# The 64-to-128 step of the triangular inverse in one PSUM bank: three rounds of four matrices instead of two bursts of eight

## The chip, the cores and the metric

The kernel runs on one core of a Trainium2 chip. Its metric is the device time of one execution in microseconds. Before the change three runs gave a median of 1597.19 us (1596.48 to 1598.59).

## The reference

One layer of a decoder for 256 tokens of width 2048, in float32. A condition vector gives shift, scale and gate; the normed input `h` is multiplied by one wide matrix `W_in`, and its columns go to two branches:

```
h = RMSNorm_pre(x) * (1 + scale) + shift
[gdn_qkv | gdn_a | gdn_b | gdn_z | ml_qk | ml_v | ml_i | ml_f | ml_o | ml_z | g_A | g_B] = h W_in
y_A = W_pA( RMSNorm_head(GatedDeltaNet(conv(q, k, v), decay, beta)) * silu(gdn_z) )
y_B = W_pB( sigmoid(ml_o) * RMSNorm_head(mLSTM(conv(q, k), v, i, f)) * silu(ml_z) )
out = (sigmoid(g_A) * y_A + sigmoid(g_B) * y_B) W_out
x <- x + gate * RMSNorm_post(out)
```

The change is in the gated delta net (32 value heads of 128, 16 query/key heads). For each head and chunk a unit lower triangular system is solved:

```
lower = where(strict, (k beta) k^T * decay, 0)
sol   = triangular_solve(lower + I, [v beta | k beta exp(g_cum)])
```

The kernel computes the inverse of such a matrix and multiplies with it. It works on chunks of 128 tokens, so the matrix is 128x128. Inverse means here: 32-blocks by substitution, then blocks of 64 from those, then the 128x128 from its two 64-blocks A and B on the diagonal and the block C that couples them, where the new block is −B⁻¹ C A⁻¹. The last is two products of 64x64 for each matrix.

## The kernel before, in words

**The stream.** Nearly all work of TensorE (PE) is products of `h` with weights that are read once. A weight unit is a 1 MB load `raw` on SP's queue (L164, three buffers). It is used in two pieces of 128x1024: ACT rounds each to `whi` (L169), DVE (POOL for some early ones) makes `wlo` = raw − whi (L170), with a ring of four pieces, and PE multiplies in three terms (hi·hi, hi·lo, lo·hi; `mm3`, L227). In a `pt` stretch these are 24 matmuls of 256 columns to a step, in a `pn` stretch 12 of 512.

**The side work.** After each piece, a step, `Side.step()` lets every side generator issue its next piece of work. All engines take their work in the order in which the program issues it; a tile scheduler adds the semaphores. The generators that matter here, for each group of four heads (`zg` 0 to 7, eight matrices of 128x128 in a group):

- `gdn_stage1` (twice per group): convolution and SiLU of q and k (`conv_silu`: ACT L651, DVE L657); load of the decay rows `gb` on SP (L675); masks on POOL (L682, L704); exponentials on ACT (L690–692); Gram products `psa`, `psb` on PE; norms and scaled matrices `au` on DVE (L738–749); the coupling values written out as `ud` (L773).
- `base_inverse`: 32-blocks by substitution on DVE, a chain of L800 (products), L804 (reduction) and L806 for 16 pairs of rows; then the result goes out to DRAM and back in another arrangement: one store `xd` (L809) and, once it has landed, four loads `xcmp` (L813), all on SP's queue. Five steps later DVE transposes and copies it (L817, L822), and ACT copies it (L820) into `x0`, `y0`.
- `gdn_stage2`: products `mp` and `mx` (32-blocks to 64), then the two products of this change: `mq` (L872), for eight matrices one burst from rows 0–63 into PSUM partitions 64–127, which ACT negates into `p2` (L874); a step later `mz` (L881), from rows 64–127 into partitions 0–63, which ACT copies into `x0` (L882). Then `pa`, `pb`, `pc`, `po` use the inverse.

While group zg is in `gdn_stage2`, `base_inverse` of the next group and `gdn_stage1` run beside it.

**What sets the order.** A number, `side.debt`, is the planner's account of DVE time that has been issued beside the stream. Each step takes 1.6 off it, never below zero; work adds to it (1.45 for a channel of the convolution) or gives back where PE's burst takes longer than usual. `base_inverse` asks `side.room(us)` before each of its L800 and L804, which yields step after step until the debt leaves room:

```python
STEP_US = 1.6
ROOM_US = 2.5
    def step(self):
        self.debt = max(0.0, self.debt - STEP_US)
    def room(self, us):
        while self.debt > 0 and self.debt + us > ROOM_US:
            yield
        self.debt += us
```

Four PSUM banks (`gtile`, tag "g") are shared by the side work; `banks(n)` yields until the next n are free, `gfree` gives one back.

Of the kernel before, what the change touches and what calls it, by code (L numbers as in the profile page):

```python
# [9 lines left out]
AF = mybir.ActivationFunctionType  # L10
# [107 lines left out]
def hybrid_layer_kernel(  # L118
# [25 lines left out]
    V, A, T, G, SP = nc.vector, nc.scalar, nc.tensor, nc.gpsimd, nc.sync  # L144
# [53 lines left out]
    def gtile(nm, held=False):  # L198
        i = slots[0] % 4
        slots[0] += 1  # L200
        t = pg.tile([P, 512], F32, name=nm, tag="g")
        freed[i] = 1 << 30 if held else side.t + 1
        slots[1][id(t)] = i, t
        return t

    def gfree(t):
        freed[slots[1].pop(id(t))[0]] = side.t

    def banks(n):

        while any(freed[(slots[0] + j) % 4] >= side.t for j in range(n)):
            yield
# [16 lines left out]
    side = Side()  # L229
# [546 lines left out]
    def base_inverse(zg, res, zr):  # L776
# [48 lines left out]
        while zg < 7 and side.t < res["t"] + STAGE2_STEPS - 1:  # L825
            yield
        side.add(gdn_stage2(zg, res, zr), 0)

    def gdn_stage2(zg, res, zr):
# [3 lines left out]
        def um(m):  # L833
            return au[m // 4][:, m % 4 // 2, 256 + 384 * (m % 2):384 + 384 * (m % 2)]
# [8 lines left out]
        for m in range(8):  # L843
            for t in range(2):
                r, o = 64 * t, 64 * t + 32
                T.matmul(pss[t][o:o + 32, m * 32:(m + 1) * 32], um(m)[r:r + 32, o:o + 32], yc[r:r + 32, m],
                         start=True, stop=True)
# [8 lines left out]
        for m in range(8):  # L856
            T.matmul(psx[0][32:64, S + m * 32:S + (m + 1) * 32], xc[32:64, m], pc_[32:64, m], start=True, stop=True)
            for t in (1, 0):
                r, o = 64 * t, 64 * t + 32
                T.matmul(psx[t][r:r + 32, m * 32:(m + 1) * 32], pc_[o:o + 32, m], xc[o:o + 32, m],  # L860
                         start=True, stop=True)
        A.activation(y0[32:64, :, 0:32], cols32(psx[0], S)[32:64], AF.Copy, scale=-1.0)
        for t in range(2):
            r = 64 * t
            A.activation(x0[r:r + 32, :, r + 32:r + 64], cols32(psx[t])[r:r + 32], AF.Copy, scale=-1.0)
            gfree(psx[t])
        yield
        yield from banks(1)
        psp = gtile("mq", True)
        side.debt -= 1.0  # L870
        for m in range(8):
            T.matmul(psp[64:128, m * 64:(m + 1) * 64], um(m)[0:64, 64:128], y0[:, m], start=True, stop=True)  # L872
        p2 = bp.tile([P, 8, 64], F32, name="p2", tag="p2", bufs=1)
        A.activation(p2[64:128], psp[64:128].rearrange("p (m i) -> p m i", m=8), AF.Copy, scale=-1.0)  # L874
        gfree(psp)
        yield
        yield from banks(1)
        psz = gtile("mz", True)
        side.debt -= 1.0
        for m in range(8):  # L880
            T.matmul(psz[0:64, m * 64:(m + 1) * 64], p2[64:128, m], x0[64:128, m, 64:128], start=True, stop=True)  # L881
        A.copy(x0[0:64, :, 64:128], psz[0:64].rearrange("p (m i) -> p m i", m=8))  # L882
        gfree(psz)
        yield

        rr = res["rr"].rearrange("p b z (h d) -> p b (z h d)", h=2)
        ys = bp.tile([P, 2, 512], F32, name="ys", tag="ys", bufs=1)
# [587 lines left out]
```

## Time and profile before

| what | us |
|---|---|
| median of three runs | 1597.19 |
| the profiled execution | 1597.11 |
| its span (first to last instruction) | 1595.1 |
| PE busy | 1581.4 |
| DVE, ACT, POOL busy | 1146.5, 937.1, 250.6 |

The granted clock of TensorE is 0.998 over the span. The rows of a timeline give start and length of an instruction (or of a run of equal ones, with their count) in us from the span's start, its engine, its line, operation, and the tile that it writes and those it reads, with types and shapes. In square brackets stands the engine's idle time just before, and what ended it. SPq is SP's queue: the length is that of issuing the transfer, not of the transfer. The table of windows has, for each stretch, its length, the busy time (and count of instructions) of PE, PE's weight loads, DVE, ACT and POOL, the granted clock, the mean share in which the 16 DMA engines were busy, and the GB/s.

The side work of one group takes some 81.6 us: the `gb` loads that the second and third group's base inverse have ahead of POOL's masks are issued at 576.26 and 657.89 us, the next at 739.51.

### The profile page before, as it was taken

Reading aid. Unit: us, or ns where it says so; the run is one execution under the profiler, and the core shown is the slowest. Engines: PE = TensorE matmul, PEld = TensorE weight load, DVE = VectorE, ACT = ScalarE, POOL = GpSimd, SP = SyncE. Lnnn points to the kernel's source line nnn. Section 1 sums busy time; section 2 is a strip of 40 time slices with the busy share of each in tenths; the row PEclk is TensorE's granted clock in tenths of the full one; section 3 lists DMA queues with packets and bytes.
Section 4 is the critical chain, followed back from the end, with each engine's and each line's share of the span. In section 5 each row is a group of like instructions: output and inputs, shape, how many; then the busy total and the mean of one; then the engine's idle time right before and its main releaser. Section 6 shows DMA issues by size and latency. Waiting matters only on the chain.

```text
span 1595.1 us, 25488 instructions
## 1 busy us (share of the span) xinstructions
PE 1581.4 (99%) x9854; PEld 1389.0 (87%) x9854; DVE 1146.5 (72%) x1804; ACT 937.1 (59%) x1494; POOL 250.6 (16%) x206
## 2 busy tenths in 40 slices
PE   8999999999999999999999999999999999999998
PEld 5888888899999999999999999889988878888886
DVE  6776556765689788888878888775768766756654
ACT  7755446765666575757576766665566554444443
POOL 5787761000000010000000000000000000100100
PEclk9999999999999999999999999999999999999999
DMA  9998775965565546555646465546778878766573
GB/s 378 393 387 320 268 295 181 297 234 181 189 190 188 189 156 206 167 182 171 193 159 207 154 195 174 187 165 232 279 268 308 320 275 295 282 248 236 206 274 108
DMA packets 96067, 372.37 MB, mean 233 GB/s; under 512 B 26021, under 2 KB 45877, under 8 KB 58185
## 3 DMA queue, kind: packets, MB, share of 16 engines
q1 hardware_dynamic: 95848, 370.65, 66.4%
q8 instruction: 77, 1.26, 0.3%
q14 instruction: 44, 0.36, 0.1%
q0 software_dynamic: 96, 0.09, 0.0%
q10 hardware_dynamic: 2, 0.01, 0.0%
HBM read 354.40 MB, written 16.31 MB: 232 GB/s over the span
## 4 chain that ended last, share of the span: by engine, by line
PE 84%; issue 12%; DMA 1%; POOL 1%; ACT 0%; DVE 0%; SPq 0%; DVEq 0%; ACTq 0%; POOLq 0%
PE pn L227 37%; PE pt L227 29%; PE py L227 8%; POOL mg L1265 1%; PE psa L227 1%; DMA raw<-in_dram 1%; PE mz L881 1%; PE mq L872 1%; PE csil L297 0%; PE po L922 0%; PE pa L893 0%; PE po L921 0%; PE pc L911 0%; PE po L919 0%; PE pb L901 0%
## 5 line engine op out<-in xcount | busy, mean ns | idle before, releaser
L170 DVE TENSOR_TENSOR wlo<-raw,whi 128x1024 fp32r<-128x1024 f32 x451 | 554.2, 1237 | 264.1 <-ACT whi L169 262.6
L169 ACT CAST whi<-raw 128x1024 fp32r<-128x1024 f32 x516 | 532.2, 1046 | 308.1 <-PE pn L227 154.4
L227 PE MATMUL pt<-h_hi,whi 128*128 128x256 f32 x1280 | 367.8, 287 | 0.0
L227 PE MATMUL pt<-h_hi,wlo 128*128 128x256 f32 x1280 | 362.1, 283 | 0.0
L227 PE MATMUL pt<-h_lo,whi 128*128 128x256 f32 x1280 | 362.0, 283 | 0.0
L227 PE MATMUL pn<-whi,h_hi 128*128 128x512 f32 x896 | 353.0, 394 | 0.3 <-ACT h_hi L169 0.3
L227 PE MATMUL pn<-wlo,h_hi 128*128 128x512 f32 x896 | 349.4, 390 | 1.5 <-POOL wlo L170 1.5
L227 PE MATMUL pn<-whi,h_lo 128*128 128x512 f32 x896 | 349.2, 390 | 0.0
L227 PEld LDWEIGHTS pt<-h_hi,whi 128*128 128x128 f32 x1280 | 245.3, 192 | 1.4
L227 PEld LDWEIGHTS pt<-h_lo,whi 128*128 128x128 f32 x1280 | 245.4, 192 | 0.3
L227 PEld LDWEIGHTS pt<-h_hi,wlo 128*128 128x128 f32 x1280 | 245.2, 192 | 0.0
L227 PEld LDWEIGHTS pn<-wlo,h_hi 128*128 128x128 f32 x896 | 168.4, 188 | 36.6 <-POOL wlo L170 2.7
L227 PEld LDWEIGHTS pn<-whi,h_hi 128*128 128x128 f32 x896 | 168.3, 188 | 35.4 <-ACT h_hi L169 1.1
L227 PEld LDWEIGHTS pn<-whi,h_lo 128*128 128x128 f32 x896 | 168.2, 188 | 35.4
L170 POOL TENSOR_TENSOR wlo<-raw,whi 128x1024 fp32r<-128x1024 f32 (+1 forms) x65 | 150.2, 2321 | 47.8 <-ACT whi L169 47.6
L227 PE MATMUL py<-whi,yhi 128*128 128x512 f32 x384 | 150.7, 392 | 0.0
L227 PE MATMUL py<-whi,ylo 128*128 128x512 f32 x384 | 149.6, 390 | 0.0
L227 PE MATMUL py<-wlo,yhi 128*128 128x512 f32 x384 | 149.5, 389 | 0.0
L473 DVE TENSOR_TENSOR part<-pn,part 128x512 f32<-128x512 f32 x112 | 73.8, 686 | 45.5 <-PE pn L227 45.3
L169 ACT CAST yhi<-ya 128x512 fp32r<-128x512 f32 x48 | 29.9, 622 | 127.8 <-PE py L227 110.9
L657 DVE SCALAR_TENSOR_TENSOR qs<-pt,gcv,qs 128x255 f32<-128x255 f32 (+2 forms) x192 | 92.2, 480 | 4.6
L170 DVE TENSOR_TENSOR ylo<-ya,yhi 128x512 fp32r<-128x512 f32 x48 | 33.2, 691 | 75.4 <-ACT yhi L169 75.4
(269 smaller groups left out, 1810.6 us busy)
## 6 DMA issues: line engine op xcount, KB each, us to landing
raw<-in_dram SPq DMA_DIRECT2D x259, 1024.0 KB
ar<-in_dram SPq DMA_DIRECT2D x31, 1024.0 KB
raw<-in_dram SPq DMA_DIRECT2D x16, 512.0 KB
ya<-o_dr SPq DMA_DIRECT2D x32, 256.0 KB
gate_dr<-part SPq DMA_DIRECT2D x11, 512.0 KB
gb<-rows SPq DMA_DIRECT2D x20, 256.0 KB
raw<-in_dram SPq DMA_DIRECT2D x6, 768.0 KB
ug<-ud SPq DMA_DIRECT2D x32, 128.0 KB
```

The source lines that it names most:

```text
L169: A.copy(hi, src)
L170: (eng or V).tensor_tensor(lo, src, hi.bitcast(F32), op=ALU.subtract)
L227: T.matmul(ps, l, r, start=start and i == 0, stop=stop and i == 2, skip_group_check=True)
L473: V.tensor_tensor(part[g][:, b], ps[b], part[g][:, b], op=ALU.add)
L657: V.scalar_tensor_tensor(dst[:, n, sh:], src[:, 0:S - sh], taps(n, 3 - sh), dst[:, n, sh:], op0=ALU.mult, op1=ALU.add)
L872: T.matmul(psp[64:128, m * 64:(m + 1) * 64], um(m)[0:64, 64:128], y0[:, m], start=True, stop=True)
L881: T.matmul(psz[0:64, m * 64:(m + 1) * 64], p2[64:128, m], x0[64:128, m, 64:128], start=True, stop=True)
L1265: G.tensor_tensor(mcols(b, hf, cg), mcols(b, hf, cg), s_, op=ALU.add)
```

## The change

The two bursts become three rounds, a step apart, all in one bank `mqz` that is held until the last. Round 0 has the first products (`mq`) of matrices 0 to 3. Round 1 alternates second products (`mz`) of matrices 0 to 3 with first products of matrices 4 to 7. Round 2 has the second products of matrices 4 to 7. ACT evacuates halves: four instructions of 64x256 instead of two of 64x512. The account `side.debt` gets 0.5 back in each of three rounds instead of 1.0 in each of two. One `yield` more stands in `gdn_stage2`, so `pa` and what follows it there come one step later.

```diff
-        psp = gtile("mq", True)
-        side.debt -= 1.0
-        for m in range(8):
-            T.matmul(psp[64:128, m * 64:(m + 1) * 64], um(m)[0:64, 64:128], y0[:, m], start=True, stop=True)
+        psq = psz = gtile("mqz", True)
         p2 = bp.tile([P, 8, 64], F32, name="p2", tag="p2", bufs=1)
-        A.activation(p2[64:128], psp[64:128].rearrange("p (m i) -> p m i", m=8), AF.Copy, scale=-1.0)
-        gfree(psp)
-        yield
-        yield from banks(1)
-        psz = gtile("mz", True)
-        side.debt -= 1.0
-        for m in range(8):
-            T.matmul(psz[0:64, m * 64:(m + 1) * 64], p2[64:128, m], x0[64:128, m, 64:128], start=True, stop=True)
-        A.copy(x0[0:64, :, 64:128], psz[0:64].rearrange("p (m i) -> p m i", m=8))
-        gfree(psz)
-        yield
+        for i in range(3):
+            side.debt -= 0.5
+            first, second = slice(4 * i, 4 * i + 4), slice(4 * i - 4, 4 * i)
+            for m in range(4 * i, 4 * i + 4):
+                if i > 0:
+                    T.matmul(psz[0:64, (m - 4) * 64:(m - 3) * 64], p2[64:128, m - 4], x0[64:128, m - 4, 64:128],
+                             start=True, stop=True)
+                if i < 2:
+                    T.matmul(psq[64:128, m * 64:(m + 1) * 64], um(m)[0:64, 64:128], y0[:, m], start=True, stop=True)
+            if i > 0:
+                A.copy(x0[0:64, second, 64:128], psz[0:64].rearrange("p (m i) -> p m i", m=8)[:, second])
+            if i < 2:
+                A.activation(p2[64:128, first], psq[64:128].rearrange("p (m i) -> p m i", m=8)[:, first], AF.Copy,
+                             scale=-1.0)
+            if i == 2:
+                gfree(psq)
+            yield
```

After the edit `mz` is L877 and `mq` L880, and the lines after the loop carry numbers greater by 4. Where the middle round lies in PE's order, in the third group: before, a burst of `mz` at that place, between the stream's `pt` and the Gram products `psa`:

```order
L227 MATMUL pt_6823<-h_hi,whi 128x256
L227 MATMUL pt_6823<-h_lo,whi 128x256
L227 MATMUL pt_6823<-h_hi,wlo 128x256
L881 MATMUL mz<-x_2798,p_6927 64x64 x8
L227 MATMUL psa<-qh 128x512
L227 MATMUL psa<-ql,qh 128x512
```

The same place now, where that burst has become pairs:

```order
L227 MATMUL pt_6825<-h_hi,wlo 128x256
L877 MATMUL mqz<-x_2798,p_6921 64x64
L880 MATMUL mqz<-y_2799,au 64x64
L877 MATMUL mqz<-x_2798,p_6921 64x64
L880 MATMUL mqz<-y_2799,au 64x64
...
L227 MATMUL psa<-qh 128x512
```

In the last listing two more such pairs are left out. The eight matmuls stand where `mz` x8 stood; the four first products are where `mq` x8 was, 24 stream matmuls ahead, and the last four follow 24 stream matmuls behind the Gram products.

On DVE, the end of the next group's `base_inverse` among the convolutions (L657) and the stream's `wlo` (L170), before:

```order
L800 TENSOR_TENSOR tmp<-xx,ug 128x8x32
L804 TENSOR_REDUCE xx<-tmp 128x8
L170 TENSOR_TENSOR wlo<-raw,whi 128x1024
L657 SCALAR_TENSOR_TENSOR qs<-pt_5833,gcv,qs 128x255
L657 SCALAR_TENSOR_TENSOR qs<-pt_5833,gcv,qs 128x254
L657 SCALAR_TENSOR_TENSOR qs<-pt_5833,gcv,qs 128x253
L170 TENSOR_TENSOR wlo<-raw,whi 128x1024
L938 SCALAR_TENSOR_TENSOR so<-so,eq 128x8
L657 SCALAR_TENSOR_TENSOR qs<-pt_5834,gcv,qs 128x255
L657 SCALAR_TENSOR_TENSOR qs<-pt_5834,gcv,qs 128x254
L657 SCALAR_TENSOR_TENSOR qs<-pt_5834,gcv,qs 128x253
L170 TENSOR_TENSOR wlo<-raw,whi 128x1024
```

The same stretch now, from the row ahead of the second of those `wlo`:

```order
L800 TENSOR_TENSOR tmp<-xx,ug 128x8x32
L170 TENSOR_TENSOR wlo<-raw,whi 128x1024
L657 SCALAR_TENSOR_TENSOR qs<-pt_5835,gcv,qs 128x255
L657 SCALAR_TENSOR_TENSOR qs<-pt_5835,gcv,qs 128x254
L657 SCALAR_TENSOR_TENSOR qs<-pt_5835,gcv,qs 128x253
L804 TENSOR_REDUCE xx<-tmp 128x8
L170 TENSOR_TENSOR wlo<-raw,whi 128x1024
L942 SCALAR_TENSOR_TENSOR so<-so,eq 128x8
```

The second listing's first `wlo` is the second of the first listing. (Tile numbers differ between the kernels: `pt_5834` of the first is `pt_5835` of the second.) The last reduction, which stood ahead of the first listing's first `wlo`, now stands ahead of its third, two steps later.

On SP, the store `xd` and the loads `xcmp` that follow from that reduction, before:

```order
L773 DMA ud<-au 32x4x32 x4
L164 DMA raw<-in_dram 128x2048 x2
L809 DMA xd<-xx 128x8x32
L813 DMA xcmp<-xd 32x1x256 x4
L164 DMA raw<-in_dram 128x2048 x2
L675 DMA gb<-rows 128x512
L164 DMA raw<-in_dram 128x2048 x3
```

The same rows of SP now:

```order
L773 DMA ud<-au 32x4x32 x4
L164 DMA raw<-in_dram 128x2048 x3
L809 DMA xd<-xx 128x8x32
L813 DMA xcmp<-xd 32x1x256 x4
L164 DMA raw<-in_dram 128x2048
L675 DMA gb<-rows 128x512
L164 DMA raw<-in_dram 128x2048 x3
```

One `raw` load has changed from behind `xcmp` to ahead of `xd`; `gb` keeps its place. The same holds in the second to the seventh group; in the first and the last group SP's order is as before. Further on, DVE's L817 and L822 now stand behind L738–743 of `gdn_stage1`, where they stood ahead of them, and ACT's L820 behind the first cast (L169) that follows the exponentials, where it stood ahead of them.

## The prediction

> **What bounds the kernel now.** I read the page first (busy times, then the chain of work that ended last), then timelines of each engine around one group of heads.
>
> ```profile
> span 1595.1 us, 25488 instructions
> PE 1581.4 (99%) x9854; PEld 1389.0 (87%) x9854; DVE 1146.5 (72%) x1804; ACT 937.1 (59%) x1494; POOL 250.6 (16%) x206
> PE 84%; issue 12%; DMA 1%; POOL 1%; ACT 0%; DVE 0%; SPq 0%; DVEq 0%; ACTq 0%; POOLq 0%
> ```
>
> PE is busy for 99% of the span, and the chain is PE plus PE's issue. So PE's sequence of matmuls is the time. A change counts in two ways: it makes that sequence shorter or longer, or it makes an operand come too late for it. The other engines have idle time, so the second happens only where one particular wlo piece is short of slack.
>
> **The edited matmuls.** This is PE's timeline around the `mq` burst of the first group, and the same row from a window that was cut at 532.1; then the busy time of `mx`, a burst that runs in several tiles.
>
> ```profile
> 530.98 0.28 PE L227 MATMUL pt<-h_lo,whi 128*128 128x256 f32 x1
> 531.10 0.28 PE L227 MATMUL pt<-h_hi,wlo 128*128 128x256 f32 x1
> 531.31 1.14 PE L872 MATMUL mq<-y,au 64*64 64x64 f32 x16
> 532.38 0.39 PE L227 MATMUL pt<-h_hi,whi 128*128 128x256 f32 x1
> 532.60 0.28 PE L227 MATMUL pt<-h_lo,whi 128*128 128x256 f32 x1
> ...
> 531.31 0.97 PE L872 MATMUL mq<-y,au 64*64 64x64 f32 x13
> ...
> 527.60:528.14 0.54, 0.52 (x48) 0.52 (x48) 0.00 (x0) 1.00 1.01 243
> ```
>
> Two `pt` matmuls start 0.12 us apart (531.10 − 530.98). From 531.10 to 532.60 there would be two such steps; there are 1.50 us, so the burst costs 1.50 − 0.24 = 1.26 us. The program's 8 matmuls show as 16 records. Three records more take 1.14 − 0.97 = 0.17 us, so 0.057 each. 16 of these are 0.91; the other 0.35 is paid for entering and leaving the 64x64 bursts, whatever their length. `mz` has the same shape, so both together cost 2.52 us.
>
> After the change there are three bursts, of 8, 16 and 8 records, and the three entries cost 1.05. In the middle one `mz` (rows 64–127) and `mq` (rows 0–63) take turns. The row of `mx` says what that may give: 48 records of three tiles in 0.52 us, 0.011 each instead of 0.057. So tiles do overlap, there into two banks. If the pairs overlap fully, the middle burst takes 8 steps: 24 × 0.057 + 1.05 = 2.42 us, 0.10 less than before. If they don't: 32 × 0.057 + 1.05 = 2.87, 0.35 more. With 8 groups: **−0.8 us** or **+2.8 us**. I take −0.8, as `mx` is the nearest row.
>
> The Trainium skill, "TensorEngine Tiling (Array Packing)", Gotcha 1, speaks against that: different row tiles cannot access one PSUM bank at the same time. That the program puts both into one bank is new; the +2.8 would follow, and no trace of before shows the case. Its Key Properties also say that a change of tiling mode drains TensorE; the 0.35 agrees.
>
> ACT's two evacuations become four of half the width:
>
> ```profile
> L874 ACT ACTIVATE p<-mq x8: 592/592/595, 532.5 to 1083.7; 64x512 f32<-64x512 f32 x8
> ```
>
> Four take between 1.2 us (half the width, half the time) and 2.4, so ACT gets 0 to 1.2 us more per group, on an engine that is idle 41% of the span. There are at least 24 `pt` matmuls (2.9 us) between one round and the next; the copy is done long before. The first reader of the result, `pa`, comes one step later, still behind its operand. PE's other bursts stay at their places between the stream's matmuls. All this: 0.
>
> **What else moves.** The three rounds give the planner back 0.5 each, 1.5 in all, where 2.0 were given back before, and a step later. `base_inverse` of the *next* group runs alongside; it issues its vector operations only when the planned debt leaves room (`side.room`). So its last reduction L804 slips two steps in the six groups from the second to the seventh, and with it the `xd` and `xcmp` transfers on SP slip past one more `raw` load (orders above). This is the main term. First DVE's rows with the reduction, then SP's queue, both in the third group's base inverse, and last the 0.4 us from 648.2 in the table of windows, where the DMA share is the figure before the last.
>
> ```profile
> 648.13 0.42 DVE L804 TENSOR_REDUCE xx<-tmp 128x8 f32<-128x256 f32 x1
> ...
> 651.03 1.22 DVE L170 TENSOR_TENSOR wlo<-raw,whi 128x1024 fp32r<-128x1024 f32 x1
> ...
> 652.24 1.51 DVE L657 SCALAR_TENSOR_TENSOR qs<-pt,gcv,qs 128x255 f32<-128x255 f32 x3
> ...
> 644.01 0.35 SPq L164 DMA_DIRECT2D raw<-in_dram  x1
> 648.58 0.38 SPq L809 DMA_DIRECT2D xd<-xx  x1
> 650.91 3.15 SPq L813 DMA_DIRECT2D xcmp<-xd  x4
> 654.16 3.64 SPq L164 DMA_DIRECT2D raw<-in_dram  x2
> 657.89 0.38 SPq L675 DMA_DIRECT2D gb<-rows  x1
> ...
> 648.20:648.60 0.40, 0.40 (x6) 0.40 (x5) 0.40 (x2) 0.20 (x1) 0.00 (x0) 1.00 0.06 21
> ```
>
> The `raw` issued at 644.01 has moved by 648.2, after which the DMA share is 0.06. Into these empty engines `xd` goes out from 648.58 to 648.96; SP waits until it has landed, at 650.91, which is 1.9 us, and issues `xcmp` until 654.06. Then come two `raw` and `gb`, which gdn_stage1 needs. The second `raw` is issued at 657.80 − 0.33 = 657.47. After the change:
>
> - The reduction stands behind the three convolutions at 652.24, which end at 653.75; with its 0.42 it ends at 654.2.
> - One `raw` now stands ahead of `xd`. Its buffer is free with the wlo that ends at 652.25, so it is issued then; from the lone load, 648.2 − 644.0 = 4.2 us, its data runs to 656.5.
> - `xd`, issued at 654.2, has to share the queue. The `ud` stores show what that means (the SP row, then the DMA packets of 676.0–678.5 and of 678.6–679.6):
>
> ```profile
> 675.59 1.75 SPq L773 DMA_DIRECT2D ud<-au  x4
> ...
> DMA packets 100, 0.82 MB, mean 328 GB/s; under 512 B 0, under 2 KB 0, under 8 KB 0
> ...
> DMA packets 603, 0.19 MB, mean 188 GB/s; under 512 B 588, under 2 KB 588, under 8 KB 588
> ```
>
> Issued from 675.59 on, none of their small packets ran before 678.5, while the 8 KB packets of the `raw` ahead of them did; then 588 came within 1 us. So `xd` starts at about 656.5. It lands between 1.0 (that microsecond) and 1.9 us later; I take 1.4: 657.9. (The Trainium skill, "DMA: Bandwidth & Descriptors", Queues, rings and completion order, states that descriptors of one ring are consumed in ring order; the trace agrees.)
> - `xcmp` takes 3.15, the one remaining `raw` is issued at 661.1, `gb` behind it.
>
> Before, from that second `raw` to the first use of `gb` on POOL were 663.02 − 657.47 = 5.55 us (next fence). So POOL starts at 666.7: **`gb` is 3.7 us late.** Who waits for that:
>
> ```profile
> 663.02 0.96 POOL L682 TENSOR_SCALAR_AFFINE_SELECT dd<-gb 128x256 f32<-128x256 f32 x2 [8.92 <-DMA gb<-rows]
> ...
> 659.85 1.69 ACT L820 COPY x<-xcmp 32x256 f32<-32x256 f32 x4
> ...
> 667.77 2.02 ACT L169 CAST whi<-raw 128x1024 fp32r<-128x1024 f32 x2
> ...
> 664.31 0.43 DVE L817 STREAM_TRANSPOSE ycmp<-xcmp 128x256 f32<-128x256 f32 x1
> 664.78 0.58 DVE L822 COPY y<-ycmp 32x256 f32<-32x256 f32 x2
> ...
> 668.87 1.23 DVE L170 TENSOR_TENSOR wlo<-raw,whi 128x1024 fp32r<-128x1024 f32 x1 [2.26 <-ACT whi L169]
> 670.01 0.28 DVE L738 SCALAR_TENSOR_TENSOR au<-psa,con 128x128 f32<-128x128 f32 x1
> ...
> 671.11 1.22 DVE L170 TENSOR_TENSOR wlo<-raw,whi 128x1024 fp32r<-128x1024 f32 x1
> ...
> 672.82 0.39 PE L227 MATMUL pn<-wlo,h_hi 128*128 128x512 f32 x1
> ...
> 675.54 0.39 PE L227 MATMUL pn<-wlo,h_hi 128*128 128x512 f32 x1
> ...
> 673.56 1.22 DVE L170 TENSOR_TENSOR wlo<-raw,whi 128x1024 fp32r<-128x1024 f32 x1
> 679.14 0.39 PE L227 MATMUL pn<-wlo,h_hi 128*128 128x512 f32 x1
> ```
>
> POOL's masks feed the exponentials on ACT (L690), and ACT works in order: behind them stand its casts. The cast at 667.77 makes whi, DVE the wlo that ends at 670.10, and PE needs it at 672.82. That is a slack of 2.72 us, and the chain from `gb` to it has no idle time. With `gb` 3.7 late PE **stalls 3.7 − 2.72 = 1.0 us**. The next piece is needed at 675.54 (now 676.5). Its wlo comes after the one now ending at 673.8, the L738 block (1.1, from 670.01 to 671.11), the transpose and copies L817/L822 (1.05, which have slipped behind that block), and 1.22 of its own: 677.1, **0.6 more**. ACT's four copies L820 (1.69) slip behind the first cast too and lie beside that. The third piece, ready at 674.78 for 679.14, has 4.36 us of slack and comes in time. So 1.6 us for an ordinary group; five of them: 8.0.
>
> Two places differ. In the seventh group's base inverse DVE is nearly full for 14 us (first row), and the fourth piece has only 1008.36 − 1007.45 = 0.91 us of slack:
>
> ```profile
> 996.00:1010.00 14.00, 14.00 (x68) 11.66 (x67) 13.61 (x29) 7.80 (x11) 1.52 (x4) 1.00 0.48 155
> ...
> 1006.23 1.22 DVE L170 TENSOR_TENSOR wlo<-raw,whi 128x1024 fp32r<-128x1024 f32 x1
> ...
> 1008.36 0.39 PE L227 MATMUL pn<-wlo,h_hi 128*128 128x512 f32 x1
> ...
> 576.26 1.96 SPq L675 DMA_DIRECT2D gb<-rows  x1
> 582.95 0.87 POOL L682 TENSOR_SCALAR_AFFINE_SELECT dd<-gb 128x256 f32<-128x256 f32 x2 [10.48 <-DMA gb<-rows]
> ```
>
> There the lag is 3.7 + 1.05 − 0.39 (its idle) − 0.91 = 3.4 us in all. And in the second group `gb` came 6.69 us after its issue instead of 5.13, 1.6 late already in this execution; with no slack left, such a delay is paid whole. I put 1.8 in for these (one such place, and a little). Sum: 8.0 + 3.4 + 1.8 = 13.2 of stalls, −0.8 on PE: **+12.4 us**. The profiled execution took 1597.11 us (its span and 2.0 around it), the median of the runs is 1597.19, the same: **1609.5 us**.
>
> Bounds of the stalls: with `xd` landing 1.0 us after 656.5 the lag is 3.3 and no `gb` is late by itself: 5 × 1.2 + 3.0 = 9. With 1.9 us the lag is 4.2, and two such late `gb`s: 5 × 2.1 + 3.9 + 3.6 = 18.
>
> **The rivals.** *`xd` is not held behind the `raw`.* Its packets are small, and an engine that has finished its part of the load may take them at once. Then it lands at 656.5, `xcmp` ends at 659.7, POOL starts at 665.3, 2.3 late: the first piece comes in time, the second 2.3 + 1.1 − 3.2 = 0.2 late, the seventh group costs 2.0, late `gb`s 1.5. 5 × 0.2 + 2.0 + 1.5 − 0.8 = +3.7: 1600.9. The `ud` rows speak against it. 12%.
>
> *The delay is covered, not slower.* The point is the slack: it decides at a lag of 2.7 us. If `gb`, issued at 661.5, does not wait for the 1 MB of the `raw` ahead of it, it is there after some 2.7 us (`xd`, half as large, took 2.3 from the start of its issue): POOL starts at 664.2, the lag is 1.2, and nothing is late but 0.9 us in the full stretch of the seventh group: −0.8 + 0.9, 1597.2. Against it: before, that would have been 660.6, and POOL, which waited 8.92 us for `gb` alone, started at 663.02. 9%.
>
> *The pairs don't overlap*, because they write one bank, with the stalls as forecast: 13.2 + 2.8 = +16.0, 1613.1. For it: no row shows two row tiles writing one bank. 10%. (This is the rule of Gotcha 1.)
>
> *Each change of tile in the middle burst is paid like an entry*, since operands alternate between halves: the 0.35 of a burst has two sides, so some 0.17 for 7 changes, 1.2 us per group, 9.6 in all and no overlap: 13.2 + 2.8 + 9.6 = +25.6, 1622.7. `mx` changes tiles every record without that. 5%.
>
> **How the numbers follow.** The forecast has 64%, with 1605 to 1615 as its own range; the rivals 12, 9, 10 and 5%. The range for all is 1598 to 1618: it leaves out the covered case and the last rival. A measurement here tells no difference under 0.2%, 3.2 us, from no change, that is up to 1600.4. The forecast, the third and fourth rivals (79%) lie above that, and half of the first (6): slower 0.85. The other half and the covered case are 15: same 0.12, and 0.03 for faster, for which no row shows more than 0.8 us.
>
> **What would show it.** In the changed kernel's profile: POOL's L682 in the periods after 550 us starts 3 to 5 us later against the stream than before; PE has idle time put down to DVE's wlo, 1 to 2 us in each of six periods and 3 to 4 in the last; `xd` waits for its landing longer than 1.9 us; the middle burst lasts about as long as 8 records of `mq` took twice, 0.5 us, when the tiles overlap, and 0.9 when they don't. I am wrong if L682 keeps its place, or comes late with PE never waiting; then the slack was larger than one row says.

## The result, and the profile after

The changed kernel takes 1639.61 us (median of 4 runs, 1639.5 to 1640.65) where the kernel before takes 1597.26: a ratio of 1.0266, 95% interval 1.0253 to 1.0279. That is 42.4 us slower. The forecast was 12.4 us slower, with a range of 1598 to 1618. The sign was right, the size was not, by a factor of more than three.

The page of the changed kernel (span, busy time, and the chain that ended last, by engine and by line):

```profile
span 1637.7 us, 25503 instructions
PE 1595.0 (97%) x9854; PEld 1391.3 (85%) x9854; DVE 1144.3 (70%) x1804; ACT 938.2 (57%) x1510; POOL 246.7 (15%) x206
PE 67%; issue 14%; DVE 6%; DMA 6%; ACT 5%; POOL 2%; SPq 1%; DVEq 0%; ACTq 0%; POOLq 0%
```

PE had 84% of the chain before; now DVE, DMA, ACT and POOL hold 19% of it. PE's own waits in the changed kernel, from the table of waits (total us, times, longest), without the rows that stand in both kernels and three small ones:

```profile
PE pn L227 <- ACT whi L169: 12.4, 6, 2.8
PE po L926 <- ACT ys L916: 8.9, 6, 1.5
PE pn L227 <- DVE wlo L170: 5.2, 8, 0.8
...
PE mpt L1069 <- ACT oT L968: 0.9, 1, 0.9
```

and all of PE's waits in the kernel before:

```profile
PE csil L297 <- ACT ar L295: 3.7, 1, 3.7
PE pn L227 <- POOL wlo L170: 1.5, 2, 0.8
PE pn L227 <- ACT h_hi L169: 0.3, 1, 0.3
```

None of the four stood there before. The first row is the late piece that was forecast, in six groups, and six of the eight waits of the third row are the `wlo` of that same piece. The second row was not forecast: `po` waits for `ys`, six times as well. The timeline of PE in the third group's period shows a third loss (starts, lengths, and idle time before in brackets):

```profile
682.32 0.39 PE L227 MATMUL pn<-whi,h_lo 128*128 128x512 f32 x1
684.52 0.50 PE L227 MATMUL pn<-whi,h_hi 128*128 128x512 f32 x1 [1.81 <-ACT whi L169]
685.78 0.50 PE L227 MATMUL pn<-wlo,h_hi 128*128 128x512 f32 x1 [0.76 <-DVE wlo L170]
...
686.57 0.46 PE L227 MATMUL pn<-wlo,h_hi 128*128 128x512 f32 x1
...
687.26 0.63 PE L227 MATMUL pn<-whi,h_hi 128*128 128x512 f32 x1
...
690.22 0.40 PE L227 MATMUL pn<-wlo,h_hi 128*128 128x512 f32 x1
...
686.00:690.50 4.50, 4.50 (x14) 3.52 (x14) 4.32 (x13) 4.13 (x7) 0.70 (x1) 0.62 0.66 233
```

A `pn` matmul normally starts 0.23 us after the one ahead of it. From 682.32 to 684.52 that is 1.97 us too late, from 684.52 to 685.78 another 1.03: a stall of 3.0 us. Then, from 686.57 to 690.22, nine steps from start to start take 3.65 us instead of 2.04. In the last row, of the table of windows, the granted clock of this stretch is 0.62. So the stall is followed by 1.6 us lost to a slower PE.

Both gaps belong to one piece: PE waits for its `whi`, runs one matmul, and waits for its `wlo`. DVE has the next piece's `wlo` ready at 687.85 + 1.23 = 689.08. At the normal pace PE would have needed it at about 688.6; slowed, it needs it at 690.22 and doesn't wait. In the fourth group, where no matmul is slow after a stall of 3.4 us, PE does wait for that second piece, 0.5 us at 777.49.

In this period: 1.65 at `po`, 3.0 at the late piece, 1.6 behind it, 6.25 us. Over the six periods the rows give: `po` 8.9 of idle time, 9.9 with the restart (by which a gap is longer than the idle time and the normal step together); the late piece 12.4 + 5.2 of idle time and 14 restarts of 0.16 to 0.27 us, together about 20.6; the clock, 0.993 in the mean instead of 0.998, 0.005 × 1637.7 = 8.2; `mpt` 0.9; less 0.8 for the pairs. That is 38.8 of the 42.4 us. Of the other 3.6, the table of waits has 1.7 in small rows: 0.9 more than before at `csil` (L297), and 0.4 each at DVE's L473 and in `py`. About 2 us are in no row that I can point to.

**The late piece.** SP's queue, POOL, ACT, DVE in the third group's base inverse and period, of the changed kernel; then the Gram product's first matmul, which is at the same place of PE's order in both kernels (before, then after):

```profile
665.42 0.38 SPq L809 DMA_DIRECT2D xd<-xx  x1
669.30 2.77 SPq L813 DMA_DIRECT2D xcmp<-xd  x4
672.17 0.38 SPq L164 DMA_DIRECT2D raw<-in_dram  x1
672.65 0.38 SPq L675 DMA_DIRECT2D gb<-rows  x1
...
678.89 0.76 POOL L682 TENSOR_SCALAR_AFFINE_SELECT dd<-gb 128x256 f32<-128x256 f32 x2 [10.52 <-DMA gb<-rows]
...
683.39 1.07 ACT L169 CAST whi<-raw 128x1024 fp32r<-128x1024 f32 x1
...
684.50 1.23 DVE L170 TENSOR_TENSOR wlo<-raw,whi 128x1024 fp32r<-128x1024 f32 x1 [7.54 <-ACT whi L169]
```

```profile
662.72 0.40 PE L227 MATMUL psa<-qh 128*128 128x512 f32 x1
...
672.68 0.40 PE L227 MATMUL psa<-qh 128*128 128x512 f32 x1
```

At the Gram products the changed kernel is 9.96 us behind. Taking that off, POOL starts at 668.93 instead of 663.02: **`gb` is 5.9 us late**, where 3.7 were forecast. With the slack of 2.72 us that makes 3.2; PE stalled 3.0. The microsecond in which the `raw` ahead of `gb` goes out, before and then after (table of windows; the DMA share is the figure before the last):

```profile
657.00:658.00 1.00, 1.00 (x11) 1.00 (x10) 0.44 (x1) 0.97 (x3) 0.00 (x0) 1.00 1.00 418
...
672.00:673.00 1.00, 1.00 (x10) 0.96 (x9) 1.00 (x2) 0.98 (x2) 0.00 (x0) 1.00 0.19 57
```

Before, the DMA engines were busy with the `raw` issued earlier; now they are nearly idle when this `raw` is issued, and so its start-up is in the chain.

**`po`.** ACT in the same period, changed kernel (first fence) and before (second); in the first, PE's `po` and DVE's `wlo` at the end:

```profile
648.36 0.84 ACT L762 ACTIVATE rr<-psv,sk 128x256 f32<-128x256 f32 x2 [9.54 <-PE pc L915]
649.09 1.05 ACT L169 CAST whi<-raw 128x1024 fp32r<-128x1024 f32 x1
650.03 1.58 ACT L651 ACTIVATE qs<-pt,gcv 128x256 f32<-128x256 f32 x4
651.46 1.08 ACT L169 CAST whi<-raw 128x1024 fp32r<-128x1024 f32 x1
652.39 0.63 ACT L916 COPY ys<-pc 128x512 f32<-128x512 f32 x1
...
653.08 0.49 PE L926 MATMUL po<-ys,au 128*128 128x128 f32 x2 [1.49 <-ACT ys L916]
...
650.17 1.22 DVE L170 TENSOR_TENSOR wlo<-raw,whi 128x1024 fp32r<-128x1024 f32 x1 [5.21 <-ACT whi L169]
```

```profile
637.27 0.84 ACT L762 ACTIVATE rr<-psv,sk 128x256 f32<-128x256 f32 x2 [6.66 <-PE pc L911]
638.00 1.05 ACT L169 CAST whi<-raw 128x1024 fp32r<-128x1024 f32 x1
638.93 0.60 ACT L912 COPY ys<-pc 128x512 f32<-128x512 f32 x1
...
639.08 1.22 DVE L170 TENSOR_TENSOR wlo<-raw,whi 128x1024 fp32r<-128x1024 f32 x1 [2.54 <-ACT whi L169]
```

L762 scales the transposed values of a later group into `rr`. That tile has two buffers, and the one it writes is free only when `pc` has read the group two before. ACT works in order, so it stands there until `pc` is done. `pc` now comes one step later, while L762 stands at its old place in ACT's order: 9.54 us instead of 6.66, 2.88 more, which is one step of 24 `pt` matmuls. Behind it two things are late. One is the cast at 649.09, and DVE idles 5.21 us instead of 2.54 in the middle of `base_inverse`. The other is `ys`, which stood directly behind one cast and now stands behind a cast, the four convolution copies and another cast, as these belong to the step in which it is now issued; it ends at 653.02, and PE's `po`, which PE would have reached at 651.43, waits 1.65 us.

### The profile page after: what moved, and what is told of

Its sections match the earlier page's. It is cut to its first block, busy times and chain, and to the rows that moved or that the text cites. A ratio compares the mean times of both kernels' runs of the same rounds, so it can differ in the third digit from the quotient of the medians.

```text
span 1637.7 us, 25503 instructions
## 1 busy us (share of the span) xinstructions
PE 1595.0 (97%) x9854; PEld 1391.3 (85%) x9854; DVE 1144.3 (70%) x1804; ACT 938.2 (57%) x1510; POOL 246.7 (15%) x206
## 3 DMA queue, kind: packets, MB, share of 16 engines
q8 instruction: 77, 1.26, 0.3%
## 4 chain that ended last, share of the span: by engine, by line
PE 67%; issue 14%; DVE 6%; DMA 6%; ACT 5%; POOL 2%; SPq 1%; DVEq 0%; ACTq 0%; POOLq 0%
PE pn L227 30%; PE pt L227 23%; PE py L227 6%; DVE wlo L170 3%; DMA gb<-rows 2%; DMA ya<-o_dr 2%; ACT whi L169 2%; POOL mg L1269 1%; DVE qs L657 1%; ACT qs L651 1%; POOL wlo L170 1%; DMA raw<-in_dram 1%; PE mqz L877 1%; DVE tmp L800 1%; SPq L813 1%
## 5 line engine op out<-in xcount | busy, mean ns | idle before, releaser
L170 DVE TENSOR_TENSOR wlo<-raw,whi 128x1024 fp32r<-128x1024 f32 x451 | 554.9, 1238 | 310.3 <-ACT whi L169 305.9
L169 ACT CAST whi<-raw 128x1024 fp32r<-128x1024 f32 x516 | 531.4, 1046 | 273.3 <-PE pn L227 131.5
L227 PE MATMUL pn<-whi,h_hi 128*128 128x512 f32 x896 | 356.9, 398 | 13.0 <-ACT whi L169 12.4
L227 PE MATMUL pn<-wlo,h_hi 128*128 128x512 f32 x896 | 353.7, 395 | 6.9 <-DVE wlo L170 5.2
L170 POOL TENSOR_TENSOR wlo<-raw,whi 128x1024 fp32r<-128x1024 f32 (+1 forms) x65 | 150.1, 2320 | 49.8 <-ACT whi L169 49.8
L169 ACT CAST yhi<-ya 128x512 fp32r<-128x512 f32 x48 | 29.9, 622 | 127.9 <-PE py L227 109.4
L473 DVE TENSOR_TENSOR part<-pn,part 128x512 f32<-128x512 f32 x112 | 73.4, 684 | 41.6 <-PE pn L227 41.6
L657 DVE SCALAR_TENSOR_TENSOR qs<-pt,gcv,qs 128x255 f32<-128x255 f32 (+2 forms) x192 | 92.1, 480 | 4.6
L170 DVE TENSOR_TENSOR ylo<-ya,yhi 128x512 fp32r<-128x512 f32 x48 | 33.1, 691 | 75.8 <-ACT yhi L169 75.7
```

The costliest lines, as they stand in the source:

```text
L169: A.copy(hi, src)
L170: (eng or V).tensor_tensor(lo, src, hi.bitcast(F32), op=ALU.subtract)
L227: T.matmul(ps, l, r, start=start and i == 0, stop=stop and i == 2, skip_group_check=True)
L473: V.tensor_tensor(part[g][:, b], ps[b], part[g][:, b], op=ALU.add)
L657: V.scalar_tensor_tensor(dst[:, n, sh:], src[:, 0:S - sh], taps(n, 3 - sh), dst[:, n, sh:], op0=ALU.mult, op1=ALU.add)
```

## The experiments

All times are compared with the kernel before on the same chip in the same job (1597.1 to 1597.2 us).

**The planner's credits alone.** The kernel before with less credit at the two bursts, chosen such that SP's order becomes that of the changed kernel.

```diff
         psp = gtile("mq", True)
-        side.debt -= 1.0
+        side.debt -= 0.8
...
         psz = gtile("mz", True)
-        side.debt -= 1.0
+        side.debt -= 0.8
```

> The kernel before, with 0.8 given back to the planner in place of 1.0 at each of the two bursts; matmuls and steps as before, while SP's order is word for word that of the changed kernel (three raw ahead of xd, one behind xcmp). Theory: this is the loss by the late gb alone. Without the step that holds ACT the lag should be the forecast's 3.7 us against a slack of 2.7: 1.0 + 0.6 us for each of six groups, a little more in the last, no drop of PE's clock after so short a stall: +9 to +14, 1606 to 1611. Rival (the slip of base_inverse alone makes the whole loss seen at the late piece, 4.8 us in each of six groups): +29, 1626. Rival (gb's delay is covered): 1597.

Measured: 1638.24 us, ratio 1.0258 (95% interval in brackets, here and below) [1.0244, 1.0272], +41.0. That is the first rival, and more than it. PE's waits:

```profile
PE pn L227 <- ACT whi L169: 19.2, 6, 3.9
...
PE pn L227 <- DVE wlo L170: 3.1, 6, 0.8
```

SP in the third group, and ACT's rows behind the exponentials:

```profile
659.05 0.43 SPq L809 DMA_DIRECT2D xd<-xx  x1
664.50 2.77 SPq L813 DMA_DIRECT2D xcmp<-xd  x4
...
678.75 1.66 ACT L820 COPY x<-xcmp 32x256 f32<-32x256 f32 x4
680.44 3.88 ACT L169 CAST whi<-raw 128x1024 fp32r<-128x1024 f32 x4
```

`po` doesn't wait here. So a change of 0.2 in each of two numbers of the planner, with not one matmul moved, costs as much as the whole change. `xd` lands 5.0 us after its issue has ended, as a `raw` was issued just ahead of it. POOL's masks start at 674.25, with PE 5.68 behind the kernel before at the Gram products: `gb` is 5.5 us late without any help from ACT's hold. My theory that the hold is needed for the late `gb` is wrong. And the stall is larger than the 3.0 us seen above, because here the copies L820 (1.66 us) still stand ahead of the first cast: 5.5 + 1.66 − 2.72 = 4.4, and the rows show 4.2 to 5.1 us in the six groups, with 1.7 to 2.4 us of slow matmuls behind it.

**The rounds and the step, without the slip.** The changed kernel with each credit at the step where it was before (so 0.8, 0.8, 0.8 and 2.4 move one step ahead of `pa`, `pb`, `pc`, `po`).

```diff
-            side.debt -= 0.5
+            side.debt -= (1.0, 1.0, 0.8)[i]
...
         pa = gtile("pa", True)
-        side.debt -= 0.8
...
         A.copy(ys[:, 1], pc)
         gfree(pc)
+        side.debt -= 2.4
         yield
         yield from banks(2)
-        side.debt -= 2.4
```

> The changed kernel's three rounds and its extra step, but each credit to the planner given at the step where the kernel before gave it; SP's order is word for word that of before. Theory: what is left is the loss at po, which waits for ys because ACT is held at L762 until pc, a step later: 1.75 us in each of six groups, less 0.8 for the overlapped pairs: +9.7, 1607. DVE's loss of 2.7 us behind the held cast may make xd and gb 2.7 us late, the edge of the slack: up to +4 on top, 1611. Rival (only the planner's credits cost): 1596.4. Rival (the new bursts cost by themselves): 1620 or more.

Measured: 1609.27, ratio 1.008 [1.0066, 1.0093], +12.1. As the theory had it; neither rival. PE's waits now have `po`, 1.1 us at `pc` and 0.9 at `mpt` once each, and no late piece of the stream beyond 0.2 us:

```profile
PE po L927 <- ACT ys L917: 8.9, 6, 1.5
```

The losses don't add up: 41.0 and 12.1 are 53, the change costs 42.4. The rows put this down to L820's place in ACT's order in the first of the two: its stalls are longer by about as much, and more matmuls are slow behind them.

**ACT's hold.** The changed kernel with L762 one step later.

```diff
         block_rows(res, z)
         yield
+        if z == 0:
+            yield
         for blk in range(2):
             A.activation(res["rr"][:, blk, z], psv[:, blk * S:(blk + 1) * S], AF.Copy, scale=sk[:, blk:blk + 1])
```

> The changed kernel with the scaled copies of gdn_stage1 (ACT L762, for the first of a group's two calls) issued one step later, so that ACT doesn't stand at them until pc is done; SP's order as in the changed kernel. Theory: the stall at po goes (6 x 1.75 = 10.5), the casts behind L762 come in time, DVE doesn't idle 5.2 us, xd goes out earlier, and the late piece costs only the forecast's 1.6 a group without a clock drop: 1597 + 12 = 1604 to 1612. Rival (hold of ACT isn't what feeds the late gb): the stall at po goes alone, 1629. Rival (neither): 1640.

Measured: 1632.37, ratio 1.0223 [1.0208, 1.0239], 7.2 us less than the change. Near the first rival's 1629: the stall at `po` falls from 1.65 to 0.70 in each of six groups (`ys` still stands behind the convolution's copies and a cast), and the late piece stays. That the late `gb` needs the hold is refuted a second time.

**Three rounds in two steps.** The alternating pairs, but without the extra step and without the slip: the last four second products go behind the Gram products in the step of the pairs, and DVE copies their result.

```diff
...
+        def last():
+            four(2)
+            gfree(psq)
+            return
+            yield
...
+        side.debt -= 1.0
+        four(0)
+        side.add(last(), 1.5)
+        yield
+        side.debt -= 1.0
+        four(1)
+        yield
```

> The three rounds in one bank with the alternating pairs, but in two steps: the last four second products are issued behind the Gram products and transposes of the step that has the pairs, and DVE copies their result. Credits, pa, and everything behind are where they were before; SP's order is that of before. Theory: the pairs overlap and nothing else changes: 8 x -0.1 = -0.8, 1596.4, the same within what can be measured. Rival (the pairs in one bank, or the held bank, cost time): 1600 or more.

Measured: 1597.48, ratio 1.0001 [0.9992, 1.001], no difference. In the last two groups, which have no Gram products in that step, PE waited for ACT's copy between the two rounds:

```profile
1024.73 0.67 PE L876 MATMUL mqz<-x,p 64*64 64x64 f32 x8 [0.86 <-ACT p L883]
```

That is 1.0 us with the restart, in each of the two groups. A version that leaves the last two groups as they were:

> e7_two_steps, but the last two groups, which have no Gram products in the step of the pairs and so stalled 1.0 us each on ACT's copy, keep the two bursts of the kernel before. Theory: 6 x -0.13 = -0.8 on PE, no stall: 1596.4, the same within what can be measured, the gain to be read from PE's positions in the trace alone. Rival: 1598 or more.

Measured: 1596.46, ratio 0.9996 [0.9987, 1.0005]. The expected 0.8 us less, which this measurement can't tell from nothing. It is the form in which the edit does no harm; it is not shown to be faster.

**The pairs themselves.** The changed kernel with the middle round's matmuls grouped.

```diff
-            for m in range(4 * i, 4 * i + 4):
-                if i > 0:
+            if i > 0:
+                for m in range(4 * i, 4 * i + 4):
                     T.matmul(psz[0:64, ...
-                if i < 2:
+            if i < 2:
+                for m in range(4 * i, 4 * i + 4):
                     T.matmul(psq[64:128, ...
```

> The changed kernel with the middle round's eight matmuls grouped (four second products, then four first products) in place of alternating; nothing else moves. Theory: only alternating neighbours overlap; the middle burst starts its 16 records 57 ns apart, 0.46 us more in each of 8 groups: +3.7 on the changed kernel, 1643. Rival (the overlap is worth nothing): 1640, the same.

Measured: 1643.59 (two runs), ratio 1.029 [1.0271, 1.0309], 4.0 us more than the changed kernel. The middle burst of the changed kernel (table of windows, `mqz` alone, then its first two records and the Gram product behind it):

```profile
536.85:537.45 0.60, 0.55 (x16) 0.54 (x16) 0.00 (x0) 1.00 0.00 0
...
536.69 0.28 PE L227 MATMUL pt<-h_hi,wlo 128*128 128x256 f32 x1
536.90 0.27 PE L877 MATMUL mqz<-x,p 64*64 64x64 f32 x1
536.90 0.27 PE L880 MATMUL mqz<-y,au 64*64 64x64 f32 x1
...
537.51 0.50 PE L227 MATMUL psa<-qh 128*128 128x512 f32 x1
```

and grouped:

```profile
535.00 0.50 PE L877 MATMUL mqz<-x,p 64*64 64x64 f32 x5
535.28 0.27 PE L881 MATMUL mqz<-y,au 64*64 64x64 f32 x1
...
535.51 0.45 PE L881 MATMUL mqz<-y,au 64*64 64x64 f32 x5
535.89 0.50 PE L227 MATMUL psa<-qh 128*128 128x512 f32 x1
```

Alternating, two records start at the same time, and the burst's first record is 0.61 us ahead of the Gram product; grouped, 0.89. The pairs do overlap, in one bank. The difference of 0.28 us is the same in all eight groups, 2.3 us in all, and less than the 0.46 expected, as some records overlap where the groups meet as well. The other 1.7 of the 4.0 us are not at the burst: PE's waits for the late piece are longer in this kernel (13.6 and 6.5 us instead of 12.4 and 5.2). That the time came out near the expected 1643 is in part luck.

**What makes the piece late.** Two kernels take the late `gb` away and leave the slip. In the first gdn_stage1 loads `gb` ahead of its convolution; DVE's order is that of the changed kernel. The second also has L762 a step later.

```diff
         z = p % 2
+        gb = decay_rows(2 * p)
         qs = bp.tile([P, 4, S], F32, name="qs", tag="qs")
...
-        gb = decay_rows(2 * p)
         dd = decay_mask(gb)
```

> The changed kernel with one edit: gdn_stage1 loads gb at its start, before the convolution, so that on SP it stands ahead of xd; DVE's order is word for word that of the changed kernel, so the slip of base_inverse stays. Theory: the late wlo is the late gb's, nothing else of the slip costs; the stalls before the late piece and the slow matmuls behind them go, po's 1.65 us in six groups stay: 1597 + 10 - 1 plus some 2 to 3 late in the program as in e3_account: 1606 to 1611. Rival (the slip delays the piece by DVE or by the copies L820, not by gb): 1625 or more.

Measured: 1608.97, ratio 1.0073 [1.0059, 1.0086], +11.8: one load moved gives back 30.6 of the 42.4 us. The slow matmuls behind late pieces and the late pieces are gone, and PE's waits beyond those of the kernel before are `po` (8.9, as above), 0.9 at `mpt` and 0.2 in `py`. So the slip of `base_inverse` costs nothing that can be seen but through `gb`.

> f1_gb_early with ACT's L762 one step later in addition, as in e5_l762. Theory: the two losses are separate, and this takes both away but for 0.70 us at po in six groups (e5_l762's): 1597 + 4 - 1, 1598 to 1603. Rival (a third loss sits in the change): 1605 or more.

Measured: 1602.61, ratio 1.0033 [1.0021, 1.0046], +5.4:

```profile
PE po L928 <- ACT ys L918: 3.2, 6, 0.5
```

So the two losses are separate. What is left is `po`'s 0.70 in six groups, 0.9 at `mpt` and 0.5 at `pc`, less 0.8 for the pairs, and under 1 us in no row.

The next kernel swaps two transfers of the changed kernel: `gb` directly behind `xcmp`, ahead of the one `raw`; `xd` stays late. The load, `gb = decay_rows(2 * p)`, is handed in as `at2` and runs a step later, behind `base_inverse`.

```diff
             side.debt += 1.45
+            if n == 2 and at2:
+                side.add(at2, 3)
...
-        gb = decay_rows(2 * p)
+        gb = early[0]
```

> The changed kernel with gb directly behind xcmp on SP, ahead of the one raw that stood between them; xd keeps its late place, DVE's order is word for word that of the changed kernel. Theory: the lag of 5.9 us consists of about 1.7 to 2 for xd and SP's wait, and of a lone raw's 4.2 us ahead of gb. Without the raw POOL starts about 2 us later than before, inside the slack of 2.7: the late piece costs nothing, po's stall stays, as in f1_gb_early: 1606 to 1611. Rival (SP's wait for xd alone makes gb late enough): stalls of 1 us or more at the late piece remain, 1617 or more.

Measured: 1627.69, ratio 1.0193 [1.0176, 1.021], +30.6. The rival: SP's wait for `xd` is enough. My sum of the lag was wrong again:

```profile
670.01 0.38 SPq L677 DMA_DIRECT2D gb<-rows  x1
...
674.89 0.76 POOL L684 TENSOR_SCALAR_AFFINE_SELECT dd<-gb 128x256 f32<-128x256 f32 x2 [8.68 <-DMA gb<-rows]
```

Even with no `raw` ahead of it, only the four small `xcmp` loads, `gb` takes 4.9 us from issue to use, while `raw` loads behind it move at the same time. PE is 7.78 behind at this Gram product, so the lag is 4.1 us: the `raw` ahead made 1.8 of the 5.9 where I had expected 4.2, and the late `xd` with SP's wait for it makes the rest. The stalls at the late piece are 1.5 us in three groups, without a slow matmul, and 2.9 in two, with seven and eight of them.

The last kernel makes `gb` late in the kernel before and touches nothing else: load and masks one step later, which puts one more `raw` ahead of it on SP.

```diff
-        gb = decay_rows(2 * p)
-        dd = decay_mask(gb)
...
-        yield from wait(2)
+        yield from wait(1)
+        gb = decay_rows(2 * p)
+        dd = decay_mask(gb)
...
+        yield from wait(1)
```

> The kernel before with gb and the masks issued one step later and nothing else; on SP gb stands behind one more raw, base_inverse, the bursts and DVE's order are as before. Theory: the late gb alone makes the loss, whatever made it late: behind one more raw it is over 4 us late, so PE stalls 1.5 to 3.5 us in each of six groups, with some slow matmuls where the stall is over about 2.5 us: 1610 to 1630. Rival (the loss needs the late xd or DVE's changed order): 1597 to 1600.

Measured: 1630.24, ratio 1.0208 [1.0193, 1.0223], +33.2, at the upper edge of the theory's range. In the third group POOL's masks start at

```profile
677.08 0.77 POOL L682 TENSOR_SCALAR_AFFINE_SELECT dd<-gb 128x256 f32<-128x256 f32 x2 [14.61 <-DMA gb<-rows]
```

with PE 8.36 behind at the Gram product, which makes `gb` 5.7 us late; `xd` goes out at its old place (656.95 − 8.36 = 648.59) and DVE's order is untouched. A late `gb` by itself makes the loss. (PE stalls at the late piece in seven groups here, the first among them.)

## Why the prediction failed, point by point

- **What bounds the kernel, and where it would be hit: right.** PE's sequence, and in six groups the wlo piece with 2.7 us of slack. PE waits there in six groups; elsewhere on the stream its waits grew by under 1 us in all.
- **The pairs, −0.8 us: right.** They overlap, the case of −0.8 against +2.8. Reckoned as in the prediction, with two steps behind the burst, PE's rows give 0.80 us for each of the three rounds (the middle one in the last group, where a `pt` follows it), 2.40 in all, against 2.52 before. The third and fourth rival fall. The rule of the Trainium skill ("TensorEngine Tiling (Array Packing)", Gotcha 1) does not hold as I read it for these tiles: 16 records in 0.55 us in one bank. They differ in row and in column tile, so they write other partitions of the bank.
- **"All this: 0": wrong, and the step that I missed.** I said that `pa` and what follows come one step later behind ready operands. I checked what they wait for, not what waits for them. ACT's L762 waits for `pc`, and everything on ACT's queue behind it waits too; and what is issued one step later on an engine in order also stands behind that step's other work. e3_account and f1_gb_early measure it without the late `gb`: 12.1 and 11.8 us, the gain of the pairs taken off.
- **The late `gb`: mechanism right, size wrong in two terms.** The lag was put at 3.7 us and is 5.9 (5.5 in e1_credits, without ACT's hold). Of the 2.2 missing, 1.2 is the term "from that second `raw` to the first use of `gb` 5.55 us": I took it from a `raw` that was issued behind another, whose start-up was hidden; on idle DMA engines it is 678.89 − 672.17 = 6.72. Another 1.4 is that `xd` landed later (669.30 − 9.96 = 659.34 for 657.9). The `raw` ahead of it went out late by as much (at about 663.6, so 653.6 for 652.25), and it is the `raw` that sets the landing: in e1_credits `xd` itself goes out 2.1 us earlier against the stream (659.05 − 5.68 = 653.37, here 655.46) and lands only 0.5 earlier (658.82). `xcmp` took 0.3 less than forecast (2.87 for 3.2). As only what exceeds the slack of 2.72 counts, 3.7 to 5.9 triples the stall: 1.0 to 3.0 at the first piece. The 0.6 at the second piece came true where PE was not slowed (0.5 in the fourth group). For the seventh group 3.4 us were forecast, counted at the fourth piece; its stalls come to 3.4, by luck: 3.0 at the first piece and 0.4 at the fourth, with slow matmuls in between that gave DVE time.
- **PE's clock: not in the sum.** Stalls of 1.5 us in three groups of g1_gb_before_raw did not bring it on, so the forecast's 1.0 + 0.6 might not have either; those of 3 did in five groups of six: 1.2 to 1.9 us behind the late piece, some 8 us in all.
- **Why `base_inverse` slips: right.** I named the credit, 1.5 for 2.0 and a step later. e1_credits slips with 1.6 for 2.0 and no extra step, so less credit is enough; e3_account, which has the extra step, doesn't slip when every credit keeps its step. What counts is when the account stands at what. Whether the later credit alone would do it, no run shows.
- **The rivals.** That `xd` passes the `raw`: no, it landed 3.5 us after its issue ended instead of 1.9. That `gb` passes it: no; and even with no `raw` ahead `gb` takes 4.9 us, not 2.7. The range ended at 1618, as the upper bound of the stalls (18) held neither ACT's hold nor the clock, and took the 5.55 for certain.

## What to carry to other kernels

Of a lag against a slack only the excess is paid, so a small error in the lag is a large one in the stall: take each term of the lag from a row in the same state (queue empty or full), and carry its upper bound through. When a step of side work moves, list for each engine in order not only what the moved instruction waits for but who waits for it, and what stands between it and its old neighbours. And where a planner's account sets the order, changing a burst's credit is a change of its own: keep the account's course, step by step, and look at the orders before and after.

## What the runs showed of the hardware

Two matmuls in opposite corners of the array, rows 64–127 into partitions 0–63 and rows 0–63 into partitions 64–127, ran at the same time into one PSUM bank: 16 records of 64x64 in 0.55 us, against 1.14 for 16 in one corner; from the first record to the matmul behind the burst it is 0.61 us alternating, 0.89 grouped and 1.07 in one corner.

PE's granted clock falls after short stalls: gaps of 2.20 and 1.26 us between starts, with one matmul in between, and soon eight matmuls that start 0.40 to 0.43 us apart instead of 0.23. Single gaps of 1.0 and 1.65 us did nothing of the kind, nor did 1.5 us in three groups of g1_gb_before_raw. The Trainium skill, "TensorE: Matmul & The Clock Gate", Part 1, has the clock halved after an idle window of about 3.4 us; the pitch agrees (0.427 us for 512 columns is its cold figure), but here stalls of 2.3 us in all and more brought it on, a matmul in between not counted. The size of the stall alone doesn't decide: 2.27 us did it in the first group of f3_gb_one (gaps of 1.46 and 1.26; granted clock 0.53 in the 3.6 us behind), while 3.38 us in the fourth group of the changed kernel did not (gaps of 2.58 and 1.25; 1.00 in the 4 us behind).

A load of 256 KB (`gb`) took 4.9 us from issue to its first use with only the four `xcmp` loads just ahead of it in its queue and 1 MB loads issued behind it (g1_gb_before_raw), and 6.2 with one 1 MB load ahead (the changed kernel).
